# A first key tile laid over memory that is free early, low halves on VectorE, and a norm step written with scalars: one decoder layer on one core

## The chip, the cores and the metric

The kernel runs on one core of a Trainium2 chip. Its time is the device time of one execution in microseconds; of several runs the median is taken. A profile is one further execution, recorded instruction by instruction. Engines: PE (TensorE, matrix products and transposes), DVE (VectorE), ACT (ScalarE), POOL (GpSimd) and SP, which here issues transfers only. Each engine takes its instructions strictly in the order in which they stand in its own queue.

## What is computed

One layer of a decoder, for a prompt of 1024 tokens and for 8 sequences of 4 new tokens (32 "sample" tokens) that have 8192 earlier tokens in a paged cache. Cut to what matters:

```
h  = rmsnorm(x, g_pre)                       # x * rsqrt(mean(x*x) + eps) * g
qa, ka, va, qi, ki, wi, ga, qb, kb, vb, gb = split(h @ w_in)
# index: for every query the 256 best keys
score[q, s] = sum_h wi[q, h] * relu(qi[q, h] . ki[s] / 8)     # 8 index heads of 64
# branch A: softmax attention over the 256 chosen keys; branch B: retention
y  = concat(silu(ga) * A, silu(gb) * headnorm(B)) @ w_out
x  = x + rmsnorm(y, g_post);  x = x + (p @ w_ple_up) * sigmoid(x @ w_ple_gate)
```

The sample tokens take their index scores against keys that are gathered from the pages of the cache, the prompt against its own.

## The kernel before, in words

Numbers are float32. A product that needs that accuracy is made of three: every operand is split into a high half, rounded to the format that PE multiplies fast (`F32R`), and a low half, operand minus high half; high times high, high times low and low times high are added in PSUM (lines 255 to 257 for the index and branch A projections).

**The start** (lines 200 to 640). Nine token tiles (eight of 128 prompt tokens, one of 32 sample tokens) are loaded (`load_x`), normed and transposed (`norm_x`). `norm_x` squares on ACT with a running sum (L528), calls `rstd_of` for the inverse root, scales on DVE (L530), transposes with eight PE instructions into a PSUM pair (L221), and writes the high half on ACT (L226) and the low half on DVE (L227), each in two pieces. `rstd_of` takes a square root on ACT (L237), a reciprocal on DVE (L238), and one correcting step on columns of 128 x 1: `z = y*y` (L239), `z = z*v` (L240), `z = 1.5 - z/2` (L241), `y = y*z` (L242). The same function serves nine more norms near the end.

`load_w` brings 256 columns of a weight in two halves of 512 KB (L175), makes the high half on ACT (L179) and the low half on POOL (L180); its raw tiles have two buffers, so a third half waits until a subtraction has read the first. The index key weights (72 columns, `wki`) have their own load, and both halves of theirs are made on POOL (L549, L550). SP's queue carries in order: tokens 0 and 1, the norm's gain, the unit matrix, tokens 2, the `wki` columns, the first index query weight `qi0`, tokens 3 to 5, the constants.

`project(g)` projects a group of 384 tokens, first to index keys (`use_ki`), then in four parts to index queries, which `q_stack` writes (L334 ACT, L335 DVE) to a tile `qis` of two buffers: groups 0 and 2 share one, group 1 has the other. `index_scores(qb)` then makes the scores of a block of 128 queries (L354 PE, L496 ACT, L500 DVE, L502 POOL); blocks 3 to 5 read the queries of group 1, blocks 6 and 7 those of group 2.

**The sample's index scores** (from L743). For each of 8 sequences and two halves, POOL gathers 1 MB of index keys from the cache into a tile `kx` of two buffers (L797); PE transposes it in two steps of eight (L807) into a PSUM pair, ACT copies that (`kT`, L808), PE multiplies it with the queries (L811), ACT takes the relu (`rl`, L814). Beside them runs `bisect_prompt`, which finds each prompt query's 256th best score by counting on DVE (L659) and ACT (L655), bit by bit, and the projections of branch A (`units`), which need PE alone.

**What sets the order.** The program is written in one order; a planner then places each instruction in its engine's queue by a simulated time line and the written order. So an instruction can come ahead of what was written before it when its inputs and its memory are expected free sooner. Memory is a stack of pools on two sides. A pool opened on the right, after another was closed there, lies over its memory, and each tile waits for what lay beneath it, not for the whole pool. Inside a pool the tiles lie in the order of their first calls. The pool `ix` of the index phase is closed, `bs` (for `bisect_prompt`, 8,960 bytes a partition) takes its top end, and `sx` (the sample's scores) lies below that. In `sx` the tiles come in the order of use, so that the first `kx` lies over the index keys `kih` and `kil` and a buffer of L496, all of which the last block of `index_scores` still reads.

Of the kernel before, what the change touches and what calls it, by code (L numbers as in the profile page):

```python
# [10 lines left out]
F32 = mybir.dt.float32  # L11
F32R = mybir.dt.float32r
# [4 lines left out]
ALU = mybir.AluOpType  # L17
# [5 lines left out]
NS = 32  # L23
# [6 lines left out]
QA, KA, VA, QI, KI, WI, GA, QB, KB, VB, GB = (  # L30
    0, 512, 640, 768, 1280, 1344, 1352, 1864, 2376, 2888, 3400)
# [89 lines left out]
def tile_step(ctx: ExitStack, tc: tile.TileContext, I, O):  # L121
    nc = tc.nc

    def pool(name, bufs=1, **kw):
        return tc.tile_pool(name=name, bufs=bufs, reuse_waits="tile", **kw)
# [36 lines left out]

    last_w = [None]

    def load_w(name, pieces):


        n = sum(p[1] for p in pieces)
        hi, lo = (wp.tile([128, KC, 256], F32R, tag=f"w{t}", bufs=2, name=f"w{t}_{name}") for t in ("hi", "lo"))
        raws = []  # L170
        for a in range(2):
            raw = wp.tile([128, KC // 2, 256], F32, tag="wraw", bufs=2, name=f"wraw_{name}{a}")
            c = 0
            for src, w in pieces:
                last_w[0] = nc.sync.dma_start(raw[:, :, c:c + w],  # L175
                                              src[a * 512:(a + 1) * 512, :].rearrange("(k p) c -> p k c", p=128)).ins
                c += w
            ks = slice(a * 4, (a + 1) * 4)
            nc.scalar.copy(hi[:, ks, :n], raw[:, :, :n])  # L179
            nc.gpsimd.tensor_tensor(lo[:, ks, :n], raw[:, :, :n], hi[:, ks, :n].bitcast(F32), op=ALU.subtract)  # L180
            raws.extend(raw[:, k, :n] for k in range(4))
        return hi, lo, raws

# [5 lines left out]
    def wcols(*cols):  # L189
        return [(w_in[:, c:c + n], n) for c, n in cols]  # L190
# [40 lines left out]
    def rstd_of(ss, rows, scale, name, sp):  # L231

        v = sp.tile(list(ss.shape), F32, tag="rs_v", bufs=2, name=f"rv_{name}")
        nc.vector.tensor_scalar(v[:rows], ss[:rows], scale, EPS, op0=ALU.mult, op1=ALU.add)
        y = sp.tile(list(ss.shape), F32, tag="rs_y", bufs=2, name=f"ry_{name}")
        z = sp.tile(list(ss.shape), F32, tag="rs_z", bufs=2, name=f"rz_{name}")
        nc.scalar.activation(y[:rows], v[:rows], AF.Sqrt)  # L237
        nc.vector.reciprocal(y[:rows], y[:rows])  # L238
        nc.vector.tensor_tensor(z[:rows], y[:rows], y[:rows], op=ALU.mult)  # L239
        nc.vector.tensor_tensor(z[:rows], z[:rows], v[:rows], op=ALU.mult)  # L240
        nc.vector.tensor_scalar(z[:rows], z[:rows], -0.5, 1.5, op0=ALU.mult, op1=ALU.add)  # L241
        nc.vector.tensor_tensor(y[:rows], y[:rows], z[:rows], op=ALU.mult)  # L242
        return y


# [220 lines left out]
    with pool("ix", side="right") as ix:  # L466
# [44 lines left out]
        def load_x(i):  # L511
            tb = norm_order[i]
            rows = 128 if tb < 8 else NS
            src = (I["x_prompt"][0, tb * 128:(tb + 1) * 128, :] if tb < 8
                   else I["x_sample"].rearrange("b t d -> (b t) d"))
            xt = xbuf[i if i < 6 else i - 4][:rows]
            nc.sync.dma_start(xt, src)
            return xt
# [3 lines left out]
        def norm_x(i):  # L522
# [11 lines left out]
            if i in (2, 3, 4):  # L534
                xin[i + 4] = load_x(i + 4)

        warm = ix.tile([128, 1], F32, name="warm")
        nc.vector.memset(warm, 0.0)
        nc.scalar.activation(warm, warm, AF.Sqrt)
        for i in range(2):  # L540
# [4 lines left out]
        wki = (ix.tile([128, KC, 72], F32R, name="wkih"),  # L545
               ix.tile([128, KC, 72], F32R, name="wkil"))
        raw = score[:, :KC * 72].rearrange("p (k c) -> p k c", c=72)
        nc.sync.dma_start(raw, w_in[:, KI:KI + 72].rearrange("(k p) c -> p k c", p=128))
        nc.gpsimd.tensor_copy(wki[0], raw)  # L549
        nc.gpsimd.tensor_tensor(wki[1], raw, wki[0].bitcast(F32), op=ALU.subtract)  # L550
        wt = [load_w("qi0", wcols((QI, 256)))]

        def project(g):

            proj_b(wki, 0, 72, use_ki, (g,))
            qis = ix.tile([128, 8, 384], F32R, tag="qis", bufs=2, name=f"qis{g}")
            qiss.append(qis)
            for j in range(4):
                yield
                proj_b(wt[j // 2], (j % 2) * 128, 128,  # L560
                       lambda g, pt, j=j: (q_stack(qis[:, 2 * j:2 * j + 2, :], 0.125, g, pt),
                                           q_sample_index(j, pt) if g == 2 else None), (g,))
# [3 lines left out]
            xin[i] = load_x(i)  # L566
        for i in range(3):
            norm_x(i)
        wt.append(load_w("qi1", wcols((QI + 256, 256))))
        nc.sync.dma_start(cst[:, 128:], I["const"][:, 128:CW])  # L570
        todo = list(range(3, 9))

# [172 lines left out]

    sx = sxs.enter_context(pool("sx", side="right"))

    wcol = sx.tile([128, 8], F32, name="wcol")
    wst = sx.tile([128, 8, 32], F32, name="wst")
    nc.sync.dma_start(wi_d, wi[:NS, 8, :])  # L750
    for a in range(4):
        nc.sync.dma_start(wcol[32 * a:32 * a + 32], bass.AP(tensor=wi_d.tensor, offset=wi_d.offset,
# [3 lines left out]
    pn = bank("pn", "t")  # L756
    for h in range(8):
        nc.tensor.matmul(pn[:NS, h * 32:h * 32 + 32], qsn[:, h, :], kis, start=True, stop=True)
    rn = sx.tile([NS, 8, NS], F32, name="rn")
    nc.scalar.activation(rn, pn[:NS, :256].rearrange("p (h k) -> p h k", h=8), AF.Relu)  # L760
    nc.vector.tensor_tensor(rn, rn, wi[:NS, 8, :][:, :, None].to_broadcast([NS, 8, NS]), op=ALU.mult)
    nc.vector.tensor_reduce(newsc, rn.rearrange("p h k -> p k h"), axis=AX.X, op=ALU.add)
# [4 lines left out]
    def head_sum(b, rls):  # L767
        py = bank("py")

        last_ = nc.tensor.matmul(py[96:128, :], wst[:, b, :], rls[3], start=True, stop=True)  # L770
        with tc.issue_after(last_.ins):
            for i in range(3):
                nc.tensor.matmul(py[32 * i:32 * i + 32, :], wst[:, b, :], rls[i], start=True, stop=True)
        ys = sx.tile([128, 512], F32, tag="ys", bufs=2, name="ys")
        nc.scalar.copy(ys, py)
        nc.sync.dma_start(xt_d[b], ys)
        pend.append(lambda: by_key(b, ys))

    def by_key(b, ys):
        pt = bank("pxt", "t")  # L780
        for i in range(4):
            nc.tensor.transpose(pt[:, i * 128:(i + 1) * 128], ys[:, i * 128:(i + 1) * 128], ident)
        xe = sx.tile([128, 4, 4, 4, 4], F32, tag="xe", bufs=1, name="xe")
        pv = pt.rearrange("p (r i e) -> p r i e", r=4, i=4)
        for t in range(4):
            nc.vector.tensor_copy(xe[:, t].rearrange("p i r u -> p r i u"), pv[:, :, :, t * 4:t * 4 + 4])
        nc.sync.dma_start(xs_d[:, b * 256:b * 256 + 256], xe.rearrange("p t i r u -> p (t i r u)"))

    def later():
        if pend:  # L790
            pend.pop(0)()

    for b in range(8):
        rls = []
        for a in range(2):
            kx = sx.tile([128, 2048], F32, tag="kx", bufs=2, name="kx")
            nc.gpsimd.indirect_dma_start(  # L797
                out=kx, out_offset=None, in_=pages,
                in_offset=bass.IndirectOffsetOnAxis(ap=kidx[:, a * 8 + b:a * 8 + b + 1], axis=0))
            for up in range(2):  # L800
                pt = pair("ptx")
                kT = sx.tile([128, 1024], F32, tag="kT", bufs=2, name="kT")
                for u2 in range(2):
                    for i in range(4):
                        r2 = up * 8 + i * 2 + u2
                        c0 = u2 * 512 + i * 128
                        nc.tensor.transpose(pt[:, c0:c0 + 128], kx[:, r2 * 128:(r2 + 1) * 128], ident)  # L807
                nc.scalar.copy(kT, pt)  # L808
                po = bank("pox", "t")
                for u2 in range(2):  # L810
                    nc.tensor.matmul(po[u2 * 64:u2 * 64 + 64, :], qbd[:, b, :], kT[:, u2 * 512:u2 * 512 + 512],  # L811
                                     start=True, stop=True)
                rl = sx.tile([128, 512], F32, tag="rl", bufs=6, name="rl")
                nc.scalar.activation(rl, po, AF.Relu)  # L814
                rls.append(rl)
            later()
            tickb[0] += 1.5
            while tickb[0] >= 1:
                tickb[0] -= 1
                step(bp)  # L820
            unit(1.4)
        pend.append(lambda b=b, rls=rls: head_sum(b, rls))
# [321 lines left out]
    low = C("low")  # L1144
# [391 lines left out]
    for qb in range(8):  # L1536
# [6 lines left out]
        n = (qb + 1) * 128  # L1543
        w = min(n, 256)
# [3 lines left out]
        for kv in range(2):  # L1548
# [5 lines left out]
            for i4 in range(4):  # L1554
# [4 lines left out]
                least, i = 3.0e38, 0  # L1559
                for c in range(0, n, 512):  # L1560
# [5 lines left out]
                    for x0, x1, add in ((c, cut, mask[:, OFF.get(qb, 0) + c:OFF.get(qb, 0) + cut]),  # L1566
                                        (cut, c + wc, near[:, h - 4 * kv, cut - n + 256:c + wc - n + 256])):
                        if x1 > x0:
                            nc.vector.tensor_tensor_reduce(L[:, x0:x1], s[:, x0 - c:x1 - c], add, 1.0, least,  # L1569
                                                           op0=ALU.add, op1=ALU.min, accum_out=mn[:, i:i + 1])  # L1570
                            least, i = mn[:, i:i + 1], i + 1
# [73 lines left out]
    wt = [load_w("o0", [(w_out[:, 0:256], 256)])]  # L1645
# [102 lines left out]
    for cb in range(4):  # L1748
        cur, curu = wg, wu
        cs = slice(cb * 256, (cb + 1) * 256)  # L1750
        for tb in (8, *range(8)):
            rows = 128 if tb < 8 else NS
# [58 lines left out]
```

## Time and profile before

| what | us |
|---|---|
| three runs | 1073.67, 1076.51, 1078.84 |
| median | 1076.51 |
| the profiled execution, its own time | 1065.73 |
| its span, first to last instruction | 1063.9 |
| PE busy | 991.7 (93%) |
| DVE busy | 699.8 (66%) |
| ACT busy | 504.2 (47%) |
| POOL busy | 288.1 (27%) |

A row of a time line reads: start, duration, engine, line, operation, out<-in with the names of the tiles, shape, count, and in brackets the idle time of the engine before it with what ended it. "L180" is line 180 of the kernel before. A row of a table by stage reads: stretch, its length, then for each engine busy time and instruction count, the clock granted to PE as a share of full speed, the share of the 16 transfer engines that was busy, and GB/s. A row of a list of waits reads: who waited for whom, us in total, times, the longest. A busy time includes the time in which an instruction that has been started is held up.

### The profile page before, as it was taken

How to read it: one execution, taken by the hardware profiler on the slowest of the kernel's cores; microseconds unless marked ns; L12 is line 12 of the kernel's file. 1: busy time of each engine (PE TensorE's matmuls, PEld its weight loads, DVE VectorE, ACT ScalarE, POOL GpSimd, SP SyncE). 2: the span in 40 equal slices, each digit the busy share in tenths (PEclk: the TensorE clock that was granted, in tenths of full speed). 3: DMA queues.
4: the chain of work that ended last, by engine and by line, in shares of the span. 5: the costliest groups of instructions: out<-in, count | busy, mean ns of one | idle time of the engine just before them, and what ended most of it. 6: DMA issues, size and time to landing. Idle time of an engine off the chain costs nothing.

```text
span 1063.9 us, 19686 instructions
## 1 busy us (share of the span) xinstructions
PE 991.7 (93%) x7375; PEld 838.6 (79%) x7375; DVE 699.8 (66%) x2012; ACT 504.2 (47%) x1092; POOL 288.1 (27%) x287
## 2 busy tenths in 40 slices
PE   3899998998999789999989995999999999999998
PEld 2899997676776778898788893666656899989998
DVE  6847768999401798978986957887764424874332
ACT  5445554986434356842333435656544523442211
POOL 3102223111201532423632512634340521222100
PEclk8999999999999989999989996899999999999999
DMA  8211235546343311112201425623211312432211
GB/s 291 65 60 51 79 96 169 186 145 202 126 164 111 70 40 41 37 48 87 61 24 41 119 86 149 190 79 105 75 56 47 117 41 80 148 111 82 86 37 40
DMA packets 98308, 102.24 MB, mean 96 GB/s; under 512 B 21346, under 2 KB 88386, under 8 KB 95906
## 3 DMA queue, kind: packets, MB, share of 16 engines
q1 hardware_dynamic: 92450, 74.74, 23.3%
q0 software_dynamic: 5760, 26.22, 7.9%
q8 instruction: 58, 0.95, 0.4%
q14 instruction: 40, 0.33, 0.1%
HBM read 79.25 MB, written 21.68 MB: 95 GB/s over the span
## 4 chain that ended last, share of the span: by engine, by line
PE 53%; DVE 8%; ACT 2%; DMA 2%; issue 1%; POOL 1%; SPq 0%; DVEq 0%; ACTq 0%; POOLq 0%
PE ob L1587 4%; PE ptp L1579 4%; PE pg L265 3%; PE pg L267 3%; PE pg L266 3%; PE po L265 3%; PE po L266 2%; PE po L267 2%; PE pvg L265 2%; PE pvg L266 2%; PE pvg L267 2%; PE sa L1563 2%; PE sa L1564 2%; PE pqk L265 2%; PE pqk L266 1%; PE pqk L267 1%
## 5 line engine op out<-in xcount | busy, mean ns | idle before, releaser
L1147 POOL DMA_INDIRECT kvs<-in_cache_kv,idx x64 | 63.6, 994 | 84.1 <-ACT pT L1584 44.7
L265 PE MATMUL pqk<-whi_qkb,xh 128*128 128x256 f32 x256 | 74.5, 291 | 5.5 <-DVE rp L1036 5.5
L265 PE MATMUL pvg<-whi_vgb,xh 128*128 128x256 f32 x256 | 77.4, 302 | 1.6 <-DVE need L729 1.5
L266 PE MATMUL pvg<-wlo_vgb,xh 128*128 128x256 f32 x256 | 76.6, 299 | 0.0
L267 PE MATMUL pvg<-whi_vgb,xl 128*128 128x256 f32 x256 | 75.2, 294 | 0.0
L266 PE MATMUL pqk<-wlo_qkb,xh 128*128 128x256 f32 x256 | 73.5, 287 | 0.0
L265 PE MATMUL po<-whi_o,yTh 128*128 128x256 f32 x256 | 73.1, 286 | 0.4 <-DVE yaT L1598 0.4
L267 PE MATMUL pqk<-whi_qkb,xl 128*128 128x256 f32 x256 | 73.0, 285 | 0.0
L267 PE MATMUL po<-whi_o,yTl 128*128 128x256 f32 x256 | 72.8, 285 | 0.0
L265 PE MATMUL pg<-whi_g,yTh 128*128 128x256 f32 x256 | 72.7, 284 | 0.0
L266 PE MATMUL po<-wlo_o,yTh 128*128 128x256 f32 x256 | 72.7, 284 | 0.0
L267 PE MATMUL pg<-whi_g,yTl 128*128 128x256 f32 x256 | 72.3, 282 | 0.0
L266 PE MATMUL pg<-wlo_g,yTh 128*128 128x256 f32 x256 | 72.2, 282 | 0.0
L500 DVE SCALAR_TENSOR_TENSOR score<-r,wi,score 128x384 f32<-128x384 f32 (+5 forms) x42 | 44.2, 1053 | 21.0 <-ACT r L496 19.9
L1572 ACT ACTIVATE L<-L,mn 128x128 f32<-128x128 f32 (+7 forms) x64 | 49.5, 775 | 13.7 <-DVE mn L1569 13.6
L265 PEld LDWEIGHTS pqk<-whi_qkb,xh 128*128 128x128 f32 x256 | 48.2, 188 | 9.6 <-issue 6.8
L1768 DVE TENSOR_TENSOR sgm<-pu,sgm 128x256 f32<-128x256 f32 x32 | 13.5, 423 | 61.8 <-PE pu L267 58.6
L265 PEld LDWEIGHTS pvg<-whi_vgb,xh 128*128 128x128 f32 x256 | 50.6, 197 | 3.7 <-issue 1.7
L266 PEld LDWEIGHTS pvg<-wlo_vgb,xh 128*128 128x128 f32 x256 | 50.7, 198 | 0.5
L267 PEld LDWEIGHTS pvg<-whi_vgb,xl 128*128 128x128 f32 x256 | 50.6, 198 | 0.6
L265 PEld LDWEIGHTS po<-whi_o,yTh 128*128 128x128 f32 x256 | 49.0, 191 | 2.2 <-issue 1.6
L496 ACT ACTIVATE r<-si 128x384 f32<-128x384 f32 (+5 forms) x48 | 36.3, 758 | 30.3 <-PE si L354 29.0
(540 smaller groups left out, 3262.1 us busy)
## 6 DMA issues: line engine op xcount, KB each, us to landing
wraw_qkb<-in_w_in SPq DMA_DIRECT2D x16, 256.0 KB
wraw_vgb<-in_w_in SPq DMA_DIRECT2D x16, 256.0 KB
wraw_o<-in_w_out SPq DMA_DIRECT2D x8, 512.0 KB
qas<-qas_d SPq DMA_DIRECT2D x8, 512.0 KB
xr<-in_x_prompt SPq DMA_DIRECT2D x8, 512.0 KB
wraw_g<-in_w_ple_gate SPq DMA_DIRECT2D x8, 512.0 KB
out_y_prompt<-sgm SPq DMA_DIRECT2D x32, 128.0 KB
qas_d<-qst SPq DMA_DIRECT2D x8, 384.0 KB
```

The costliest lines, as they stand in the source:

```text
L265: nc.tensor.matmul(pt[:, :n], ah, hi[:, k, :n], start=(k == 0), stop=False)
L266: nc.tensor.matmul(pt[:, :n], ah, lo[:, k, :n], start=False, stop=False)
L267: nc.tensor.matmul(pt[:, :n], al, hi[:, k, :n], start=False, stop=(k == kc - 1))
L496: nc.scalar.activation(r[:, :n], s[:, :n], AF.Relu)
L500: nc.vector.scalar_tensor_tensor(sc, r[:, :n], wi[:, qb, h:h + 1], sc, op0=ALU.mult, op1=ALU.add)
L1147: return nc.gpsimd.indirect_dma_start(out=dst, out_offset=None, in_=kvflat, in_offset=bass.IndirectOffsetOnAxis(ap=idx, axis=0))
L1563: nc.tensor.matmul(s[:, :wc], qas[:, h, :], kah[kv][:, c:c + wc], start=True, stop=False)
L1564: nc.tensor.matmul(s[:, :wc], qas[:, h, :], kal[kv][:, c:c + wc], start=False, stop=True)
L1572: behind[0] = nc.scalar.activation(L[:, :n], L[:, :n], AF.Exp, bias=least, scale=-1.0, accum_out=sm[:, i4:i4 + 1])
L1579: nc.tensor.transpose(tp[:, i4 * 128:i4 * 128 + 128], P[i4][:, kb * 128:kb * 128 + 128], ident)
L1587: nc.tensor.matmul(ob[64 * o:64 * o + 64, :256], vtok[:, kb, kv * 64:kv * 64 + 64], pT[:, o * 256:o * 256 + 256], start=(kb == 0), stop=(k ...
L1768: nc.vector.tensor_tensor(sg[:rows], usrc, sg[:rows], op=ALU.mult)
```

## The change

Four edits, all in one function:

- `rstd_of` makes `y*y*v` in one instruction that takes both factors as scalars of a partition, and the last product likewise: four DVE instructions become three.
- `load_w` can be given the engine of the low half. The two index query weights `qi0` and `qi1` take VectorE, and each half is subtracted in two pieces of 128 x 512; all other weights stay on POOL in one piece of 128 x 1024.
- `qi0` is written after the norms of the first three token tiles, just ahead of `qi1`, so also behind the loads of tokens 3 to 5. The two instructions that make `wki` are written after the second norm; its copy stays on POOL, its subtraction goes to VectorE.
- The pool `ix` takes the query tiles `qis` before its small tiles, and the pool `sx` takes its tiles in another order, the first `kx`, `kT` and `rl` last, so that these lie at its top end. They were buffers that the planner gave out in turn; they become tiles of their own, used in a fixed turn.

```
-    def load_w(name, pieces):
+    def load_w(name, pieces, low=nc.gpsimd):
...
-            nc.gpsimd.tensor_tensor(lo[:, ks, :n], raw[:, :, :n], hi[:, ks, :n].bitcast(F32), op=ALU.subtract)
+            for k in range(0, 4, 4 if low is nc.gpsimd else 2):
+                k2 = 4 if low is nc.gpsimd else k + 2
+                low.tensor_tensor(lo[:, a * 4 + k:a * 4 + k2, :n], raw[:, k:k2, :n],
+                                  hi[:, a * 4 + k:a * 4 + k2, :n].bitcast(F32), op=ALU.subtract)
...
-        nc.vector.tensor_tensor(z[:rows], y[:rows], y[:rows], op=ALU.mult)
-        nc.vector.tensor_tensor(z[:rows], z[:rows], v[:rows], op=ALU.mult)
+        nc.vector.tensor_scalar(z[:rows], y[:rows], y[:rows], v[:rows], op0=ALU.mult, op1=ALU.mult)
         nc.vector.tensor_scalar(z[:rows], z[:rows], -0.5, 1.5, op0=ALU.mult, op1=ALU.add)
-        nc.vector.tensor_tensor(y[:rows], y[:rows], z[:rows], op=ALU.mult)
+        nc.vector.tensor_scalar(y[:rows], y[:rows], z[:rows], None, op0=ALU.mult)
...
+        qfirst = ix.tile([128, 8, 384], F32R, tag="qis", bufs=2, name="qis0")
         warm = ix.tile([128, 1], F32, name="warm")
...
-        nc.gpsimd.tensor_copy(wki[0], raw)
-        nc.gpsimd.tensor_tensor(wki[1], raw, wki[0].bitcast(F32), op=ALU.subtract)
-        wt = [load_w("qi0", wcols((QI, 256)))]
+        wt = []
...
-            qis = ix.tile([128, 8, 384], F32R, tag="qis", bufs=2, name=f"qis{g}")
+            qis = qfirst if g == 0 else ix.tile([128, 8, 384], F32R, tag="qis", bufs=2, name=f"qis{g}")
...
         for i in range(3):
             norm_x(i)
-        wt.append(load_w("qi1", wcols((QI + 256, 256))))
+            if i == 1:
+                nc.gpsimd.tensor_copy(wki[0], raw)
+                nc.vector.tensor_tensor(wki[1], raw, wki[0].bitcast(F32), op=ALU.subtract)
+        wt.append(load_w("qi0", wcols((QI, 256)), nc.vector))
+        wt.append(load_w("qi1", wcols((QI + 256, 256)), nc.vector))
...
+    made = {}
+
+    def slot(tag, shape, name):
+        if tag in made:
+            return made.pop(tag)
+        return sx.tile(shape, F32, tag=tag, bufs=1, name=name)
+
     wcol = sx.tile([128, 8], F32, name="wcol")
     wst = sx.tile([128, 8, 32], F32, name="wst")
+    rn = sx.tile([NS, 8, NS], F32, name="rn")
+    made["xe"] = sx.tile([128, 4, 4, 4, 4], F32, tag="xe", bufs=1, name="xe")
+    for tag, w in (("ys0", 512), ("ys1", 512), *((f"rl{i}", 512) for i in range(1, 6)), ("kT1", 1024),
+                   ("kx1", 2048), ("rl0", 512), ("kT0", 1024), ("kx0", 2048)):
+        made[tag] = sx.tile([128, w], F32, tag=tag, bufs=1, name=tag)
+    turn = {"rl": 0, "kT": 0, "kx": 0, "ys": 0}
+
+    def ring(tag, w, n):
+        i = turn[tag] % n
+        turn[tag] += 1
+        return slot(f"{tag}{i}", [128, w], tag)
...
-            kx = sx.tile([128, 2048], F32, tag="kx", bufs=2, name="kx")
+            kx = ring("kx", 2048, 2)
...
-                kT = sx.tile([128, 1024], F32, tag="kT", bufs=2, name="kT")
+                kT = ring("kT", 1024, 2)
...
-                rl = sx.tile([128, 512], F32, tag="rl", bufs=6, name="rl")
+                rl = ring("rl", 512, 6)
```

More of the change, by code (lines that the diff above doesn't have):

```diff
@@ L758, in tile_step @@
         nc.tensor.matmul(pn[:NS, h * 32:h * 32 + 32], qsn[:, h, :], kis, start=True, stop=True)
-    rn = sx.tile([NS, 8, NS], F32, name="rn")
     nc.scalar.activation(rn, pn[:NS, :256].rearrange("p (h k) -> p h k", h=8), AF.Relu)
@@ L773, in head_sum @@
                 nc.tensor.matmul(py[32 * i:32 * i + 32, :], wst[:, b, :], rls[i], start=True, stop=True)
-        ys = sx.tile([128, 512], F32, tag="ys", bufs=2, name="ys")
+        ys = ring("ys", 512, 2)
         nc.scalar.copy(ys, py)
@@ L782, in by_key @@
             nc.tensor.transpose(pt[:, i * 128:(i + 1) * 128], ys[:, i * 128:(i + 1) * 128], ident)
-        xe = sx.tile([128, 4, 4, 4, 4], F32, tag="xe", bufs=1, name="xe")
+        xe = slot("xe", [128, 4, 4, 4, 4], "xe")
         pv = pt.rearrange("p (r i e) -> p r i e", r=4, i=4)
```

## The prediction

> **What bounds the kernel.** I read the page's totals first: PE is busy 93% of a span of 1063.9 us, so time can be won only where PE stands still or waits. Then the table by stage, for where that is, and the list of PE's waits in those stages.
>
> ```profile
> 10.00:20.00 10.00, 2.93 (x14) 2.32 (x13) 9.37 (x11) 4.97 (x10) 7.18 (x4) 0.79 1.01 341
> 20.00:30.00 10.00, 9.11 (x45) 7.46 (x43) 8.81 (x32) 6.10 (x13) 2.67 (x2) 0.70 0.55 163
> 30.00:40.00 10.00, 6.67 (x44) 5.94 (x43) 9.55 (x23) 6.99 (x16) 2.38 (x1) 1.00 0.60 173
> 40.00:50.00 10.00, 10.00 (x66) 9.68 (x65) 9.04 (x23) 5.06 (x15) 0.00 (x0) 1.00 0.00 0
> ...
> 280.00:290.00 10.00, 10.00 (x62) 7.89 (x61) 0.61 (x4) 3.78 (x7) 4.81 (x3) 1.00 0.39 133
> ```
>
> From 10 to 40 us PE works 18.7 of 30 and DVE 27.7: the start is DVE's. From 40 us PE is full, and at 280 us, still ahead of the branch in `bisect_prompt`, DVE is nearly idle while PE is full. So what PE does not lose at the start moves everything behind it.
>
> ```profile
> PE pt L221 <- DVE xl L227: 6.9, 1, 6.9
> PE pt L221 <- DVE rv_x L234: 3.1, 2, 2.9
> ```
> ```profile
> PE pox L811 <- ACT kT L808: 4.8, 1, 4.8
> PE pox L811 <- DVE vnew L414: 1.6, 1, 1.6
> ...
> PE ptx L807 <- DMA kx<-in_cache_kidx,kidx: 1.1, 1, 1.1
> ```
>
> The first list is 0 to 60 us, the second 168 to 350. The change touches the start (6.9 and 2.9) and the sample's first key tile (4.8 and 1.1).
>
> **The start: what holds DVE.** The time lines of DVE, of POOL beside it, and PE's first projection:
>
> ```profile
> 12.22 0.73 DVE L239 TENSOR_TENSOR rz_x<-ry_x 128x1 f32<-128x1 f32 x1
> 12.99 2.27 DVE L240 TENSOR_TENSOR rz_x<-rz_x,rv_x 128x1 f32<-128x1 f32 x1
> 15.30 0.15 DVE L241 TENSOR_SCALAR rz_x<-rz_x 128x1 f32<-128x1 f32 x1
> 15.49 2.08 DVE L242 TENSOR_TENSOR ry_x<-ry_x,rz_x 128x1 f32<-128x1 f32 x1
> 17.60 1.28 DVE L530 SCALAR_TENSOR_TENSOR score<-score,ry_x,mask 128x1024 f32<-128x1024 f32 x1
> ...
> 25.65 2.34 DVE L240 TENSOR_TENSOR rz_x<-rz_x,rv_x 128x1 f32<-128x1 f32 x1
> ...
> 33.28 3.47 DVE L530 SCALAR_TENSOR_TENSOR score<-score,ry_x,mask 128x1024 f32<-128x1024 f32 x1
> ```
> ```profile
> 11.51 1.43 POOL L550 TENSOR_TENSOR wkil<-score,wkih 128x576 fp32r<-128x576 f32 x1
> 12.90 4.64 POOL L180 TENSOR_TENSOR wlo_qi<-wraw_qi,whi_qi 128x1024 fp32r<-128x1024 f32 x2
> ```
> ```profile
> 22.46 0.57 PE L255 MATMUL pb<-xh,wkih 128*72 128x384 f32 x1 [0.89 <-ACT xh L226]
> ```
>
> A DVE instruction with two tensors in SBUF ends when POOL's subtraction ends: 12.95 against 12.94, 15.26 near the middle of the pair, 17.57 against 17.54. The one with one tensor (L241) takes 0.15 us amid the second subtraction. Against 0.15 for a column and 1.28 for L530 undisturbed (the row at 17.60), the stalls are 0.58 + 2.12 + 1.93 + 2.19 + 2.19 = 9.0 us. Every low half that causes them leaves POOL.
>
> **What DVE gets for it.** The nearest row by shape, the split of a token tile:
>
> ```profile
> L227 DVE TENSOR_TENSOR xl<-pt,xh 128x512 fp32r<-128x512 f32 x16 | 10.8, 682 | 1.6 <-ACT xh L226 1.5
> ```
>
> Eight pieces of 128 x 512 at 0.68 are 5.5 us, and the `wki` piece of 128 x 576 some 0.75: 6.2 us. The upper bound is POOL's own price, 1.43 for the `wki` piece and 2.32 for each half, 10.7 us; with two tensors in SBUF and nothing on POOL, DVE's row is the nearer, and I take it (at the upper bound DVE wins nothing and neither does the start). A norm loses one instruction of 0.15; no row has two scalars from memory, and if such a one costs as much as two, nothing is won: I take 0.1 for each of nine, 1 us. Net for DVE: 9.0 + 1.0 - 6.2 = 3.8 us less.
>
> Where on the path? The 4.6 us before 17.57 lie ahead of PE's first projection; behind them stand L530, eight transposes and the two casts, unchanged. So it starts at 22.46 - 4.6 = 17.9, or 18.6 if the `wki` piece comes first. Afterwards two stalls go (4.4 us) and 5.5 us of pieces come, so the PE gap at 34 to 39 us (10 - 6.67 = 3.3 us in the 30 to 40 row) about remains if DVE is the limit, and closes if the planner puts the pieces between what PE needs. The start thus gives 3.8 (DVE the limit throughout) to 7.9 us (4.6 and the whole gap). DVE's 9.55 of 10 stands nearer the first; I take 5.0.
>
> **What is moved at the start.** `qi0`'s two loads pass behind three of 512 KB on SP:
>
> ```profile
> 13.66 1.06 ACT L179 CAST whi_qi<-wraw_qi 128x1024 fp32r<-128x1024 f32 x1
> ...
> 24.47 1.03 ACT L179 CAST whi_qi<-wraw_qi 128x1024 fp32r<-128x1024 f32 x1
> ...
> 32.16 1.05 ACT L179 CAST whi_qi<-wraw_qi 128x1024 fp32r<-128x1024 f32 x1
> ```
>
> 1.5 MB at 341 GB/s are 4.6 us: the second half, cast at 13.66, is there at about 18.3, cast by 19.4, subtracted by 21. PE first projects the index keys, 24 products; the start's clock was 0.70 of full speed and the first product took 0.57 us, so that lasts at least 6 us, to 24: about 3 us of cover, and 5 if the clock stays low. Without it PE would wait by what is missing, one for one. The tokens 3 to 5 come sooner by the 1.0 MB that stood ahead, 3 us. `wki`'s copy stays on POOL, which then has nothing to hold it; it must be done by 17.9, and its columns were there at 10.28. The third and fourth half (24.47 and 32.16) need raw buffers that are now freed by DVE, in its order: a rival, below.
>
> **The sample's first key tile.** By the sizes of the tiles, the first `kx` now lies 8,960 to 17,152 bytes under the top, over the `wki` halves and the query buffer of group 1; the second lies mostly over that of groups 0 and 2.
>
> ```profile
> 128.37 0.81 ACT L496 ACTIVATE r<-si 128x768 f32<-128x768 f32 x1 [1.12 <-PE si L354]
> ...
> 169.97 1.03 ACT L496 ACTIVATE r<-si 128x1024 f32<-128x1024 f32 x1 [0.36 <-PE si L354]
> ```
> ```profile
> 173.25 1.38 POOL L797 DMA_INDIRECT kx<-in_cache_kidx,kidx  x1 [0.57 <-issue]
> 174.94 0.94 POOL L797 DMA_INDIRECT kx<-in_cache_kidx,kidx  x1 [0.31 <-PE pb L257]
> ```
>
> Block 5 (768 keys) is read at 128.4, block 7 at 170: the first gather may go some 40 us sooner, the second some 3 us. What they cost now:
>
> ```profile
> 176.00:180.00 4.00, 3.13 (x18) 2.81 (x17) 4.00 (x7) 1.16 (x2) 4.00 (x2) 1.00 0.90 332
> 180.00:184.00 4.00, 1.94 (x16) 1.73 (x16) 3.83 (x11) 0.38 (x1) 1.59 (x2) 1.00 1.01 385
> 184.00:188.00 4.00, 1.10 (x4) 0.30 (x4) 3.90 (x14) 3.40 (x6) 0.00 (x0) 0.82 0.97 277
> 188.00:192.00 4.00, 4.00 (x22) 2.21 (x19) 3.83 (x12) 4.00 (x8) 0.00 (x0) 0.76 0.55 195
> ```
> ```profile
> 184.57 1.15 ACT L655 ACTIVATE js<-mask,cand 128x1024 bf16<-128x1024 bf16 x1 [2.29 <-DVE cand L674]
> ...
> 185.84 1.01 ACT L808 COPY kT<-ptx 128x1024 f32<-128x1024 f32 x1
> ```
> ```profile
> 186.90 1.98 PE L811 MATMUL pox<-kT,qbd 128*64 128x512 f32 x4 [4.78 <-ACT kT L808]
> 188.81 1.62 PE L807 MATMUL ptx<-cst,kx 128*128 128x128 f32 x8
> 190.36 1.08 PE L811 MATMUL pox<-kT,qbd 128*64 128x512 f32 x4
> ```
>
> PE stands still for 0.87 + 2.06 + 2.90 = 5.8 us: 1.1 for the data, the rest because the copy `kT` stands on ACT behind a count that waits for DVE. With the first tile there, its transposes and two products (about 4.2 us) go before 180, and only the second tile's copies can still stand behind that count. PE would then be at its next product around 185.4, where the copy ends near 186.9: 1.5 us stay, 4.3 go. After the pause PE is also slow: the clock falls to 0.82 and 0.76; 1.98 us stand for products that take 1.08 once it is up, and eight transposes behind them take 1.62, which by the same ratio of half speed and full is some 0.5 too much: 1.4 us. A shorter pause spares that, so at most 5.7. [...]
>
> Not all of it need last. At 244 PE waits again, for a copy on DVE:
>
> ```profile
> 237.92 3.55 DVE L663 SCALAR_TENSOR_TENSOR cnt<-cnt,cst 128x2 f32<-128x2 f32 x1 [0.75 <-ACT js L655]
> ```
>
> `vnew` stands behind this stalled instruction, and DVE from 172 to 244 has its own chain. If PE comes sooner and DVE does not, the wait grows by the gain. Between 0 and 5.7 I take 3.5.
>
> **The tail.** Nine more norms lose about 0.1 us each, and PE there is fed by products for most of the time: 0.3, between 0 and 1.
>
> **Sum.** 5.0 + 3.5 + 0.3 = 8.8 us; the profiled execution would go from 1065.7 to 1056.9. It is 10.8 under the median of the runs, which are 5 apart among themselves; stalls count one for one in either, so the median goes from 1076.5 to 1067.7. About 0.5%, 5.4 us, can be told from no change here.
>
> **Rivals.**
>
> *The sample's gain is handed back* at 244, as above, or the planner leaves the gather behind the last block's mask on POOL, so that the first tile isn't early at all. For it: DVE is over 90% busy there. Against: the planner puts DVE's copies earlier too when it sees PE earlier. 5.3 us are left: 1071.2.
>
> *The subtractions hold DVE.* The third and fourth half land late (casts at 24.47 and 32.16). On POOL that cost nobody; on DVE whatever stands behind them waits, the norms of tokens 3 to 5 among it. It decides if the last half's pieces stand ahead of those norms and its cast ends later than about 25. At worst 32.16 - 24.47 = 7.7 us of DVE idle against the 3.8 won, nothing gained at the sample, and a pause that makes PE slow again. The 20 to 30 row prices that: 9.11 busy at 0.70, so 2.7 us. 1076.5 + 7.7 - 3.8 + 2.7 = 1083.1, slower. Against it: the raw buffers come free with DVE's own first pieces near 21, and from 40 us the transfers stand idle.
>
> *The clock comes up sooner.* PE now pauses for 6.9 us ahead of the third tile, and the row from 20 to 30 has 0.70. With the stalls gone that pause is about 2.3; if PE then runs at full speed from its first projection, those 2.7 us go as well: 1065.0. Against: the first tiles' transposes are few, and PE may be slow whatever the pause. [...]
>
> **Numbers.** The forecast 0.45, handed back 0.28, held DVE 0.12, clock 0.15. Predicted 1067.7. The low end takes both gains near their bounds, the clock, and some scatter: 1059; the high end no gain and the scatter of the runs, leaving out most of the slower case: 1078. Faster by over 0.5%: most of the forecast, the clock, and a third of the handed-back case, 0.64. Within: the rest of these and a mild form of the held DVE, 0.26. Slower: 0.10.
>
> **What would show it.** Right: no DVE column instruction over 0.3 us before 40 us; PE's first projection near 18; eight new DVE subtractions near 0.68; a gather near 131, before the block-6 mask; PE idle from 176 to 188 (less the shift) under 2 us. Wrong: a DVE wait for a weight's cast ahead of a norm; a wait for `vnew` of 5 us instead of 1.6; the first gather still behind the last block.

## The result and the profile after

| kernel | median us | runs | lowest, highest |
|---|---|---|---|
| before | 1076.12 | 22 | 1072.61, 1082.58 |
| after | 1081.80 | 22 | 1076.22, 1087.04 |

The ratio of after to before is 1.0054, 95% interval 1.0040 to 1.0068; measured again on another chip (below) it is 1.0052, 1.0031 to 1.0073. The kernel became slower by half a per cent; 1067.7 had been predicted, with 1059 to 1078 as the range.

The profiled execution of before that the prediction read (1065.73) lies 7 us under the fastest of these 22 runs, so the first traces of the two kernels are 16.4 us apart where their medians are 5.7. For everything behind the start I therefore compare a second pair of traces, taken on one chip: before 1069.77 (span 1068.0), after 1078.79 (span 1077.0).

**The start** did what it should. The table by stage, first trace of after; the prediction shows the same rows of before:

```profile
10.00:20.00 10.00, 6.34 (x26) 4.96 (x27) 9.25 (x26) 9.01 (x18) 1.26 (x1) 1.00 1.03 353
20.00:30.00 10.00, 10.00 (x48) 8.48 (x48) 8.83 (x29) 5.62 (x12) 0.28 (x1) 1.00 0.66 176
30.00:40.00 10.00, 9.23 (x59) 8.85 (x59) 9.17 (x24) 7.40 (x18) 0.00 (x0) 1.00 0.53 160
```

PE works 25.6 us of these 30, where it worked 18.7. The time line of DVE, and PE's first projection:

```profile
13.26 0.27 DVE L242 TENSOR_SCALAR rz_x<-ry_x,rv_x 128x1 f32<-128x1 f32 x1
13.56 0.15 DVE L243 TENSOR_SCALAR rz_x<-rz_x 128x1 f32<-128x1 f32 x1
13.75 0.21 DVE L244 TENSOR_SCALAR ry_x<-ry_x,rz_x 128x1 f32<-128x1 f32 x1
13.88 0.75 DVE L572 TENSOR_TENSOR wkil<-score,wkih 128x576 fp32r<-128x576 f32 x1
...
19.97 1.28 DVE L182 TENSOR_TENSOR wlo_qi<-wraw_qi,whi_qi 128x512 fp32r<-128x512 f32 x2
...
27.77 1.29 DVE L182 TENSOR_TENSOR wlo_qi<-wraw_qi,whi_qi 128x512 fp32r<-128x512 f32 x2 [0.54 <-ACT whi_qi L179]
...
30.63 1.29 DVE L182 TENSOR_TENSOR wlo_qi<-wraw_qi,whi_qi 128x512 fp32r<-128x512 f32 x2 [1.25 <-ACT whi_qi L179]
```
```profile
19.37 0.56 PE L257 MATMUL pb<-xh,wkih 128*72 128x384 f32 x1 [0.80 <-ACT xh L229]
```

No column instruction is stalled, the pieces cost what was forecast, and DVE waits only 0.54 and 1.25 us for a weight's cast.

**What became of it.** POOL masks the last 128 columns of each finished block of scores, and then issues the sample's gathers; their starts are marks of how far the kernel is (second pair of traces, POOL's time line, us):

| mark | before | after | difference |
|---|---|---|---|
| mask of block 2 | 76.51 | 70.68 | -5.8 |
| mask of block 3 | 95.44 | 89.05 | -6.4 |
| mask of block 4 | 113.79 | 112.60 | -1.2 |
| mask of block 5 | 131.42 | 131.56 | +0.1 |
| mask of block 6 | 152.28 | 152.28 | 0.0 |
| mask of block 7 | 173.50 | 176.16 | +2.7 |
| first gather | 174.37 | 176.83 | +2.5 |
| third gather | 183.51 | 189.16 | +5.7 |
| last gather | 323.00 | 332.46 | +9.5 |
| span | 1068.0 | 1077.0 | +9.0 |

The start wins 6 us. Five of them go between the masks of blocks 3 and 4, and 1.3 more up to that of block 5; 2.7 us are lost at the mask of block 7, 3.2 up to the third gather, and 3.8 up to the last. From there on the two run alike. Each of the first two places shows a low half of a weight that stays on POOL. Between blocks 3 and 4, POOL and DVE of before and then of after:

```profile
95.44 0.29 POOL L502 TENSOR_SCALAR_AFFINE_SELECT score<-score 128x128 f32<-128x128 f32 x1 [18.64 <-DVE wi L483]
96.37 5.48 POOL L180 TENSOR_TENSOR wlo_qa<-wraw_qa,whi_qa 128x1024 fp32r<-128x1024 f32 x2 [0.63 <-ACT whi_qa L179]
```
```profile
95.77 0.43 DVE L666 COPY mask<-score 128x512 bf16<-128x512 bf16 x1 [0.33 <-POOL score L502]
96.11 0.55 DVE L498 TENSOR_SCALAR score<-r,wi 128x640 f32<-128x640 f32 x1
```
```profile
89.05 0.29 POOL L504 TENSOR_SCALAR_AFFINE_SELECT score<-score 128x128 f32<-128x128 f32 x1 [18.08 <-DVE score L502]
89.31 4.92 POOL L182 TENSOR_TENSOR wlo_qa<-wraw_qa,whi_qa 128x1024 fp32r<-128x1024 f32 x2
```
```profile
89.37 2.62 DVE L671 COPY mask<-score 128x512 bf16<-128x512 bf16 x1 [0.40 <-POOL score L504]
...
92.47 2.10 DVE L500 TENSOR_SCALAR score<-r,wi 128x640 f32<-128x640 f32 x1
...
95.49 0.18 DVE L374 TENSOR_SCALAR qsn<-pb 64x32 f32<-64x32 f32 x1
```
```profile
95.73 0.25 PE L782 MATMUL pn<-kis,qsn 64*32 64x32 f32 x2 [1.19 <-DVE qsn L374]
96.41 0.40 PE L257 MATMUL pb<-xh,whi_qi 128*128 128x288 f32 x1 [0.43 <-DVE qsn L374]
```

In before the cast of `qa0` came late enough that the copy and the product on DVE went first: POOL began at 96.37, 0.26 us behind the start of the product. In after the cast is done earlier, and POOL subtracts from 89.31 on, 0.06 us ahead of the copy. The copy then takes 2.62 instead of 0.43, the product 2.10 instead of 0.55, the query copies behind them are late, and PE, full in before, stands. From 84 to 104 us it works 18.3 us with 113 instructions, where in before it worked all 20.0 with 142, and its clock from 96 to 104 is 0.79 instead of 1.00. Being held does not cost time everywhere: in before, sums of block 4 behind the product are held too (1.47, 1.11 and 3.05 us, where an undisturbed one takes 0.88), and PE stays full up to 104 us.

At block 7, POOL and then the waits of PE from 168 to 200 us in after; in before the gather stood right behind the mask and `ga`'s low half behind both:

```profile
173.80 2.42 POOL L182 TENSOR_TENSOR wlo_ga<-wraw_ga,whi_ga 128x1024 fp32r<-128x1024 f32 x1 [21.22 <-ACT whi_ga L179]
176.16 0.49 POOL L504 TENSOR_SCALAR_AFFINE_SELECT score<-score 128x128 f32<-128x128 f32 x1
176.83 1.14 POOL L820 DMA_INDIRECT kx<-in_cache_kidx,kidx  x1 [0.18 <-issue]
```
```profile
PE ptx L830 <- DMA kx<-in_cache_kidx,kidx: 8.3, 1, 8.3
PE pox L834 <- ACT kT L831: 3.0, 1, 3.0
```

The cast of this weight runs at 172.66 instead of 175.90, and the planner has put its first low half ahead of the mask; why, its own simulated time line would have to show, and that is not on record. So the mask ends late, and with it the gathers and the bisection's first count. The second low half, behind the gathers, then holds one more step of DVE, which now stands just ahead of that count and takes 0.42 us in before:

```profile
179.71 2.35 POOL L182 TENSOR_TENSOR wlo_ga<-wraw_ga,whi_ga 128x1024 fp32r<-128x1024 f32 x1
```
```profile
179.48 2.88 DVE L778 TENSOR_TENSOR wst<-wcol,cst 128x256 f32<-128x256 f32 x1
```

PE meanwhile had little else: up to 176 us it had worked 159.0 us against 156.2, so it seems that the other products that fill this stretch in before (40 more instructions there from 176 to 196) were already done. What was left of the start's gain ended as a wait for the gather.

### The profile page after: what moved, and what is told of

Same layout as the page of the kernel before. It is cut to its first block, busy times and chain, and to the rows that moved or that the text cites. A ratio compares the mean times of both kernels' runs of the same rounds, so it can differ in the third digit from the quotient of the medians.

```text
span 1080.3 us, 19679 instructions
## 1 busy us (share of the span) xinstructions
PE 1000.3 (93%) x7375; PEld 844.1 (78%) x7375; DVE 697.6 (65%) x2003; ACT 506.5 (47%) x1092; POOL 281.5 (26%) x282
## 4 chain that ended last, share of the span: by engine, by line
PE 71%; DVE 11%; issue 8%; DMA 5%; ACT 3%; POOL 2%; SPq 1%; POOLq 0%; ACTq 0%; DVEq 0%
PE pb L257 4%; PE ob L1610 4%; PE ptp L1602 4%; PE pb L258 3%; PE pb L259 3%; PE po L267 3%; PE po L268 3%; PE po L269 3%; PE pg L267 3%; PE pg L269 3%; PE pg L268 3%; PE pvg L268 2%; PE pvg L267 2%; PE pox L834 2%; PE pvg L269 2%
## 5 line engine op out<-in xcount | busy, mean ns | idle before, releaser
L1170 POOL DMA_INDIRECT kvs<-in_cache_kv,idx x64 | 68.1, 1065 | 82.1 <-ACT pT L1607 31.1
```

Source lines behind the costliest of these rows:

```text
L1170: return nc.gpsimd.indirect_dma_start(out=dst, out_offset=None, in_=kvflat, in_offset=bass.IndirectOffsetOnAxis(ap=idx, axis=0))
```

## The experiments

Theory A: the start's gain is real, and low halves on POOL, brought into worse places by it, eat it. Theory B, the rival: the new order of memory costs the time. Four runs on one chip, before at 1070.10:

**The start alone.** All edits but the memory order:

```
-        qfirst = ix.tile([128, 8, 384], F32R, tag="qis", bufs=2, name="qis0")
...
-            kx = ring("kx", 2048, 2)
+            kx = sx.tile([128, 2048], F32, tag="kx", bufs=2, name="kx")
```

> The kernel after, with the memory of before in the index phase and in the sample's scores: only the norm's scalars, the low halves on VectorE and the moved weight stay. Theory A (the loss after 88 us comes from POOL's low halves, which the earlier start brings into worse places: the one of qa0 right behind the mask of block 3, where it holds a copy and a product on DVE for some 4 us, and the first of ga0 ahead of the mask of block 7 and of the first gather): it behaves like the kernel after, ratio to before 1.000 to 1.008, mask of block 3 near 90 and of block 4 near 115, first gather 5 to 7 us later than before's 173.25. Theory B (the new order of memory costs the time and the start is a clean gain): 4 to 6 us faster than before, ratio 0.994 to 0.996, first gather near 169.

1079.07, ratio 1.0075 (1.0048 to 1.0101). Its copy of block 3 took 2.61 us, its product 2.11; block 4's mask stood at 111.77, the first gather at 176.13, behind `ga`'s low half at 173.10. The gather came only 2.9 us later than before's 173.25, where 5 to 7 had been expected, and block 4's mask 3 us sooner than expected. But the loss is here without the new memory: B falls.

**The memory order alone**, on the kernel before:

```
+        qfirst = ix.tile([128, 8, 384], F32R, tag="qis", bufs=2, name="qis0")
...
+    for tag, w in (("ys0", 512), ("ys1", 512), *((f"rl{i}", 512) for i in range(1, 6)), ("kT1", 1024),
+                   ("kx1", 2048), ("rl0", 512), ("kT0", 1024), ("kx0", 2048)):
+        made[tag] = sx.tile([128, w], F32, tag=tag, bufs=1, name=tag)
```

> The kernel before with only the new order of memory for the query tiles and the sample's scores. Theory A: the time of before or up to 3 us less, ratio 0.997 to 1.001; the first gather stands right behind the mask of block 7, near 173, because nothing else in POOL's queue has moved, and the second near 175. Theory B: 5 to 10 us slower than before, ratio 1.005 to 1.010.

1069.72, ratio 0.9995 (0.9979 to 1.0012): no change. The first gather stands at 174.88, right behind the mask of block 7 at 174.41. By the sizes of the tiles its memory has been free for some 40 us (the last scores of block 5 are read at 130.56), but the planner leaves it where it is written.

**`ga0`'s low halves behind the first gathers**, on the kernel after:

```
+                with (tc.issue_after(got[0]) if name == "ga0" else ExitStack()):
                     low.tensor_tensor(lo[:, a * 4 + k:a * 4 + k2, :n], raw[:, k:k2, :n],
```

> The kernel after with the low halves of the weight ga0 issued behind the first two gathers, as they stood before. Theory A: mask of block 7 right behind its last score, near 176 instead of 178.4, first gather near 177, first count of the bisection at 179 to 180 instead of 184.5; 4 to 8 us less than the kernel after, ratio to before 0.997 to 1.002. Theory B: within 1 us of the kernel after, ratio 1.004 to 1.007.

1075.31, ratio 1.0040 (1.0021 to 1.0059). The mask went to 174.23, 1.4 us behind its last score's start, and the gather to 174.70, but the 4 to 8 us that had been expected did not come. What the trace shows in their place is the next held step, on DVE and POOL:

```profile
176.91 5.55 DVE L786 TENSOR_TENSOR rn<-rn,wi 32x256 f32<-32x256 f32 x1
```
```profile
177.53 4.65 POOL L184 TENSOR_TENSOR wlo_ga<-wraw_ga,whi_ga 128x1024 fp32r<-128x1024 f32 x2
```

A step of 0.41 us on DVE (its price when POOL is still, in the run with all three orders below) was held up to the end of the moved pair, and the bisection with it.

**The same, and the first gather really early**:

```
+            with (tc.high_priority() if 2 * b + a < 1 else ExitStack()):
```

> As the run before this one, and the first gather ahead of the mask of block 7, which its memory allows: it goes near 155, right behind the mask of block 6. Theory A: PE's wait for the gathered tile (7.5 us in the kernel after) goes, but the copy kT still stands on ACT behind a count; 0.5 to 4 us less than the run before this one, ratio to before 0.994 to 1.001. If the first tile's early arrival is worth nothing because the copy waits for DVE's counts anyway: within 1 us of the run before this one.

1066.73, ratio 0.9970 (0.9953 to 0.9987): 8.6 us less than the run before it, twice what I expected at most. The gather went at 153.83, behind the mask of block 6. PE's waits for gathered tiles are 0.3 us in all, and both copies `kT` of the first tile pass ahead of the count. The wait has moved to the second tile, whose copy stands behind the count:

```profile
178.90 1.93 ACT L834 COPY kT<-ptx 128x1024 f32<-128x1024 f32 x2 [0.35 <-PE ptx L833]
190.00 1.15 ACT L662 ACTIVATE js<-mask,cand 128x1024 bf16<-128x1024 bf16 x1 [9.17 <-DVE cand L681]
```
```profile
194.08 1.98 PE L837 MATMUL pox<-kT,qbd 128*64 128x512 f32 x4 [9.58 <-ACT kT L834]
```

The stretch from the mask of block 6 to the last gather is 172.5 us against 176.5 in the run before it. So the traces place 4.0 us of the 8.6; the rest they do not show, as the two traces are only 4.5 us apart in all.

Four more on a second chip, before at 1077.27.

**`qa0`'s low halves behind the copy and the product**, on the kernel after:

```
+                    if qb == 4:
+                        hold["qa0"] = [(sc0.ins, mybir.DependencyClass.Sync)]
```

> The kernel after with one wait more: the low halves of qa0 on POOL wait for the first product of block 4's scores on DVE, so also for the copy of block 3's scores that stands ahead of it. In the kernel before both had gone ahead of them by 0.2 us. Theory A: the copy takes 0.43 to 0.6 us instead of 2.62 and the product 0.55 to 0.7 instead of 2.10; the stretch from the mask of block 3 to that of block 4 falls from 23.5 to 25 us to 18 to 20; the loss at block 7 stays, so 3 to 6 us less than the kernel after, ratio to before 0.999 to 1.003. If the stretch has another cause (the products pn put in between): it stays above 22 us and the ratio at 1.004 to 1.008.

1082.03, ratio 1.0040 (1.0015 to 1.0066). The two took 0.43 and 0.55, as expected, but the stretch fell only to 21.5 us, and the time by no amount that can be told from the kernel after. The halves now hold the sums behind:

```profile
95.46 2.46 DVE L507 SCALAR_TENSOR_TENSOR score<-r,wi,score 128x640 f32<-128x640 f32 x1
...
99.73 6.77 DVE L507 SCALAR_TENSOR_TENSOR score<-r,wi,score 128x640 f32<-128x640 f32 x3
```

An undisturbed sum takes 0.88. Moved alone, a pair of 5 us meets the next victims. I had expected 18 to 20 us and 3 to 6 us of gain: the direction was right, the size wrong.

**All three orders**, with `ga0` also behind the steps that make `newsc`; the two edits above, and

```
+            if b == 0:
+                hold.setdefault("ga0", []).append((got.ins, mybir.DependencyClass.NoSync))
...
+    hold.setdefault("ga0", []).append((last_n.ins, mybir.DependencyClass.Sync))
```

> The kernel after with all three orders: qa0's low halves behind the first product of block 4, the first gather ahead of block 7's mask, ga0's low halves behind the first two gathers and also behind the four steps on DVE that make newsc (one of them, 32 x 256, stood 4.9 and 5.6 us held by these halves in the two runs that only put them behind the gathers). Theory A: mask of block 4 near 109, first gather near 149, no DVE instruction of the sample's start over 1.3 us, first bit's bound (cand) 4 to 6 us sooner after block 7's mask than the 14.8 us there; 8 to 14 us less than the kernel after, ratio to before 0.988 to 0.994. If PE is full anyway and DVE's chain only stands beside it: no better than the run with the early gather, 0.995 to 0.999.

1069.41, ratio 0.9935 (0.9908 to 0.9961). Masks of blocks 4 and 7 at 110.88 and 171.77; the step `rn` takes 0.41; the bound `cand` comes 12.0 us behind the mask, as in before and after (12.0 and 11.9), instead of 14.7 and 14.8 in the two runs that only moved `ga0` behind the gathers; 9 to 11 had been expected.

**The memory order and an early gather, without the start's edits**: the memory order alone, and

```
+            with (tc.high_priority() if 2 * b + a < 1 else ExitStack()):
```

> The kernel before with the new order of memory, and the first gather ahead of block 7's mask: the sample's edit as it was meant, with none of the start's. If the early tile is worth what was forecast (3.5 us, 0 to 5.7): ratio 0.995 to 0.999, gather near 154, PE idle from 176 to 190 down by 3 to 4 us. If it is worth as much as in the kernel after with both moves (8.6 us between the two medians): 0.991 to 0.994. If the wait only moves to the second tile's copy behind DVE's count: 0.999 to 1.001.

1073.58, ratio 0.9966 (0.9943 to 0.9990): 3.7 us between the medians, the size the prediction gave this term, but with an interval from about 1 to 6 us, and the trace does not bear the size out. Waits of PE from 168 to 200 us, first of the memory order alone, then with the early gather, and the table by stage of both:

```profile
PE pox L830 <- ACT kT L827: 5.7, 1, 5.7
```
```profile
182.00:188.00 6.00, 1.25 (x12) 1.01 (x10) 5.79 (x20) 1.75 (x4) 1.62 (x2) 0.89 1.03 362
188.00:196.00 8.00, 7.07 (x28) 3.21 (x28) 6.79 (x21) 7.97 (x14) 0.52 (x1) 0.65 0.49 175
```
```profile
PE pox L831 <- ACT kT L828: 5.0, 4, 2.2
```
```profile
182.00:188.00 6.00, 3.53 (x26) 2.24 (x23) 5.76 (x20) 2.50 (x4) 2.12 (x2) 1.00 0.76 204
188.00:196.00 8.00, 5.52 (x32) 2.78 (x33) 7.01 (x20) 8.00 (x15) 0.94 (x1) 1.00 0.84 270
```

PE waits nearly as long for `kT`, but four times instead of once, at most 2.2 us, and its clock stays at 1.00 where it was 0.89 and 0.65: it runs 58 instructions in these 14 us instead of 40. The lead does not last. Counted from the mask of block 6, the seventh gather stands at 62.5 us, 3.1 sooner than in before (65.6); the eighth at 84.4, against 84.6; the last at 171.3, against 170.7 in both traces of before and 171.7 in the memory order alone. Between the seventh and the eighth PE waits 2.9 us for a copy on ACT (`kvs`, 1.4 in before), and from 210 to 260 us its clock is 0.90 instead of 1.00. Where the 3.7 us of the medians lie is open.

**The start with `qa0` and `ga0` moved, on the old memory**: the start alone, with the edits of all three orders but for

```
-            with (tc.high_priority() if 2 * b + a < 1 else ExitStack()):
```

> The start's edits with the memory of before, with qa0's low halves behind block 4's first product and ga0's behind the first two gathers and newsc; the first gather must still wait for the last block. Theory A: the start's 4 us reach the end, ratio 0.994 to 0.998. Theory B (the start's gain goes wherever the low halves stand, since the sample's stage waits for DVE): 0.999 to 1.003.

1076.18, ratio 0.9986 (0.9962 to 1.0009): between the two expectations, not told from no change. Masks of blocks 2, 4 and 7 at 70.87, 110.73 and 171.70, so the start's gain still shrinks where sums are held, and PE then waits 4.0 us for the gather that must stand behind the last block. On this chip the start's edits with `qa0` and `ga0` moved are 1.1 us under before without the early gather and the memory that allows it, and 7.9 with both: the start needs the early gather to be worth its time.

The last four on a third chip, before at 1071.93.

**Before, unchanged, for a second trace.**

> The kernel before, unchanged, for a second trace: the mask of block 2 stood at 75.38 in its first trace, and at 77.58 and 78.03 in the two runs whose start is that of before. If the first trace had a quick start: near 77.8 here, the last gather near 325 instead of 321.85, the span 3 to 8 us over 1063.9. If those two runs lost it by their other memory: 75 to 76 here, the last gather near 322.

Block 2's mask at 76.51, the last gather at 323.00, the span 1068.0: between the two. The first trace was quick by 1.1 us at its start and by 4.1 in all. The trace is the left column of the table of marks.

**After, unchanged.**

> The kernel after, unchanged, beside the runs of this chip: ratio to before 1.003 to 1.008 as in the first measurement (1.0054); mask of block 2 near 71.5, of block 4 near 114, first gather near 178.

1077.24, ratio 1.0052 (1.0031 to 1.0073). Blocks 2 and 4 at 70.68 and 112.60, the gather at 176.83; the right column.

**POOL's low halves in four pieces**, on the kernel after:

```
-            for k in range(0, 4, 4 if low is nc.gpsimd else 2):
-                k2 = 4 if low is nc.gpsimd else k + 2
+            for k in range(0, 4, 1 if low is nc.gpsimd else 2):
+                k2 = k + (1 if low is nc.gpsimd else 2)
```

> The kernel after with every low half that stays on POOL cut in four pieces of 128 x 256, the order of all queues else nearly the same. Theory A (a DVE instruction that needs what POOL's subtraction holds waits for the end of that subtraction, up to 2.4 us, not for the end of the pair of them): the copy of block 3 takes at most 1.1 us instead of 2.62, the product 1.2 instead of 2.10, other held instructions fall alike; 3 to 8 us less than the kernel after, ratio to before 0.998 to 1.002. If DVE is held for as long as POOL subtracts, whatever the pieces: the copy still takes over 2 us and the ratio stays at 1.004 to 1.007.

1068.55, ratio 0.9980 (0.9960 to 1.0000), 8.7 us less than the kernel after beside it.

```profile
89.61 7.42 POOL L182 TENSOR_TENSOR wlo_qa<-wraw_qa,whi_qa 128x256 fp32r<-128x256 f32 x8
```
```profile
89.68 0.95 DVE L671 COPY mask<-score 128x512 bf16<-128x512 bf16 x1 [0.40 <-POOL score L504]
...
91.11 0.55 DVE L500 TENSOR_SCALAR score<-r,wi 128x640 f32<-128x640 f32 x1
...
93.49 0.88 DVE L502 SCALAR_TENSOR_TENSOR score<-r,wi,score 128x640 f32<-128x640 f32 x1
```

Nothing moved in POOL's queue: the subtraction still begins 0.07 us ahead of the copy, and POOL even works longer (7.42 for the pair against 4.92). But DVE gets in between two pieces. The stretch from block 3 to 4 falls from 23.6 to 18.9 us, and that from the mask of block 6 to the last gather from 180.2 to 176.1, where `wst` takes 0.41 us instead of 2.88. This is the plainest proof that the holding, and not the order as such, costs the time. Not all of it: the mask of block 7 is as late as before it (24.5 us behind that of block 6, against 23.9), and PE then waits 8.7 us for the gather.

**All three orders and pieces.**

> The run with all three orders, with POOL's low halves in four pieces as well. What was left there: three sums of block 4 that took 6.77 us together instead of 2.6, held by the second weight qa1. Theory A: they take under 4 us, mask of block 4 near 108.5 instead of 110.9, 1 to 4 us less than with the three orders alone, ratio to before 0.990 to 0.993. If pieces do nothing: 0.993 to 0.996.

1061.62, ratio 0.9911 (0.9889 to 0.9933), the lowest of all, though its interval overlaps that of the three orders alone; it is faster than both kernels. Block 4's mask stands at 108.30; its three sums take 2.65 us instead of 6.77, and little is still held (1.13 us for one sum, 2.35 for two). What stays is PE's wait for the second tile's copy `kT`, 6.1 us behind a count. Pieces on the kernel before were not tried, so how much of their gain is independent of the change is open.

## Why the prediction was wrong

**The start was right, two of its terms were not.** Forecast 5.0 us (3.8 to 7.9); the mask of block 2 came 3.7 us sooner in the first pair of traces and 5.8 in the second. The stalls went, the eight pieces took 0.68 to 0.69 each, no norm waited over 1.25 us for a cast. The norm's term was nothing instead of 1 us: a step with two scalars takes 0.27 and one with one 0.21, together 0.48, where three undisturbed steps of before took 0.16 each. And PE's first projection came at 19.4 instead of 17.9 to 18.6. The weight `qi0` behind three loads was covered: the pieces of both its halves, from 19.97 and 21.83 on, had no wait ahead of them.

**The step that failed** is "what PE does not lose at the start moves everything behind it", and with it the sum that lets the start's 5.0 us pass to the end. It rested on a row at 40 us and one at 280. The rule that the prediction had read from its own rows, a DVE instruction with two tensors ends when POOL's subtraction ends, was applied up to 40 us and no further: "every low half that causes them leaves POOL" is true of the stalls at the start and of no others. The change left `qa0`, `qa1`, `kava` and `ga0` on POOL, each a pair of about 5 us. Coming earlier, `qa0` met the copy and the product (2.62 and 2.10 us), and by the mask of block 4 the lead had shrunk by 5.2 us; `ga0` passed ahead of block 7's mask and cost 2.7 there. The pieces show that it is the holding: with the same order in POOL's queue they bring 8.7 us, though how much of that they would bring before as well is open. The rule itself was too narrow: the copy and the product each read one tensor and are held all the same (2.62 us instead of 0.43, 2.10 instead of 0.55), as `rn` with two is (5.55 instead of 0.41). Which began first, DVE's instruction or POOL's, does not settle it: in before the product that began 0.26 us ahead of the subtraction took its 0.55, but the record of `rn` begins 0.62 us ahead of one and was held all the same. Nor is every DVE instruction held: with all three orders four counts of 0.95, 0.82, 0.69 and 0.55 us, as long as where POOL is still, ran amid the pair at 179.04, and the next scalar step, 0.17 us long in before, took 1.79. What decides between them, no run shows.

**"The first gather may go some 40 us sooner"** was right of the memory as far as it was tried (the gather ran 21 us ahead of block 7's mask) and wrong of the queue. Left alone, it stayed behind the mask of block 7; the planner kept the written order, in the memory order alone as in the kernel after. This was one half of a rival (0.28), which however kept the start's gain. Where the gather does go early, the medians give 3.7 us without the start's edits against 3.5 forecast, but this agreement is luck as far as the trace shows: the 3.1 us won up to the seventh gather are gone at the eighth, which is the other half of that rival, at another copy than the one at 244 us that it named. Nor does any trace have a stretch from block 6's mask to the last gather clearly under before's 170.7: the run with all three orders and pieces has 170.6. With the start's edits and `ga0` moved, the early gather was worth 8.6 by the medians; what the traces show of it is that it takes back a part of what the stretch had lost (176.5 us without it, 172.5 with it). The prediction's upper bound for the sample, 5.7 us, counts on a shorter pause than 4.78 us leaving the clock up, and the runs show both: a pause of 2.92 us ahead of 37.49 in before and waits of at most 2.2 us with the memory order and the early gather left it at 1.00, pauses of 1.18 and 0.37 us in after were followed by 0.50 (last section).

**The held DVE** (0.12) ended on the right side, with 1083.1 near the measured 1081.80, by luck: there DVE waits for a late cast ahead of its own pieces, which cost 0.54 and 1.25 us; what held it were the halves that stay on POOL. **"The clock comes up sooner"** can't be told: the row from 20 to 30 us has a clock of 1.00 in after, but in the second trace of before too, with the same 9.11 us of work as the 0.70 of the first.

**The tail** can't be told: from the last gather to the end it is 745.0 us in before and 744.5 in after, but 742.1 in the first trace of before, and 0.3 had been forecast. Not explained are 1.3 us between the masks of blocks 4 and 5. The 3.8 us from the third gather to the last agree with PE's waits there (10.0 us against 5.7 from 196 to 340), the longest for a copy on ACT (4.0) and a step of the bisection (2.9); which instruction set each I did not test.

## What to carry to other kernels

When a change makes a stage earlier, list what long instructions on POOL stand in the stages behind it, and ask for each what DVE will be doing when it now begins; here 5.2 us of the start's gain went between the masks of blocks 3 and 4, where two such pairs stand (`qa`, 4.92 and 5.33 us). Cutting these instructions in four brought the copy from 2.62 to 0.95 us and the product from 2.10 to 0.55; it cost POOL a fifth more where DVE left it alone (5.55 us for the second pair of `ga` against 4.72) and half as much again where DVE got in between (7.42 against 4.92). Memory that is free early moves a transfer only if the queue lets it (free from 130.56 us on, the gather stood at 174.88): check the order as issued, ask for the early place, and then see what the time won there meets next.

## What was not expected of the hardware

PE's clock fell after two short pauses, of 1.18 and 0.37 us. First trace of after, PE and the table by stage:

```profile
96.72 0.31 PE L782 MATMUL pn<-kis,qsn 64*32 64x32 f32 x2 [1.18 <-DVE qsn L374]
97.39 0.61 PE L257 MATMUL pb<-xh,whi_qi 128*128 128x288 f32 x1 [0.37 <-DVE qsn L374]
97.80 0.44 PE L258 MATMUL pb<-xl,whi_qi 128*128 128x288 f32 x1
```
```profile
96.00:102.00 6.00, 4.92 (x21) 4.78 (x22) 5.65 (x18) 1.46 (x3) 0.00 (x0) 0.56 0.32 88
```

Between 95.5 and 97.4 us PE did only two small products. The granted clock was 1.00 from 95 to 96 us, 0.84 in the next and 0.50 from 97 to 103, and products of 288 columns took 0.44 us apiece, where they take 0.29. In the second trace of after the same two pauses (1.19 and 0.43 us) are followed by products of 0.43 and 0.44 us that start from 97.04 to 100.15, at a mean clock of 0.79 from 96 to 104 us. The prediction's estimate that a shorter pause leaves the clock up does not hold in general; what brought it down here, no run shows.
